# A decoder layer's FFN: the down projection in seven block products, with hidden values and weight forms in DRAM

## The chip, the cores and the metric

The kernel runs on one core of one Trainium2 chip, in one launch. The metric is the device time of that launch in microseconds (us); lower is better. The TensorE clock has two levels, 1.2 and 2.4 GHz; a granted clock of 1.00 in the profile is the upper one.

## What is computed

One inference step of a decoder layer on 1024 prompt tokens and 8 x 4 sample tokens, T = 1056 in all, width 1024, FFN width 2816, all in float32:

```python
m, sh, sr = _mixer(x, pos, ...)          # input projection, 4 HGRN2 heads, 4 retention heads, output projection
x = _layer_norm(ALPHA * x + m, ln1_g, ln1_b)
hidden = silu(x @ w_gate) * (x @ w_up)   # (T, 2816)
x = _layer_norm(ALPHA * x + hidden @ w_down, ln2_g, ln2_b)
```

The change lies in the FFN, that is in the last two lines.

## The kernel before

Activations stand transposed in SBUF, features over the 128 partitions and tokens along the row, in four quarters q of 264 tokens; two quarters make a half pr. A float32 product is made of three matmuls: each operand is split into a high part (a cast on ScalarE, L189) and a low part (a subtraction, L190, on GpSimd for weights and on VectorE for most else), and TensorE adds hi x hi, hi x lo and lo x hi into one PSUM tile. A matmul takes a 128 x 128 weight block and 264 columns.

The 2816 hidden features are 22 blocks of 128, worked off as 11 pairs p. For each pair the kernel computes gate and up values and then at once the pair's share of the down projection:

- Pair 0 computes gate and up plainly (`gu`).
- For pairs 1 to 10 `unit` (matmuls L910) computes gate, and again up, in the Strassen-Winograd form: the two feature blocks, the two halves of the 1024 inputs and the two quarters of a half make 2 x 2 blocks, and seven products A11 x B11, S2 x T2, S3 x T3, S1 x T1, A12 x B21, A22 x T4, S4 x B22 take the place of eight. Each product has 12 matmuls for each half, a unit 7 x 2 x 12 = 168. `blocks` loads two raw weight blocks into the three slots of `wr` and makes the block forms S1 to S4 on GpSimd (L885 to L892). The token forms T1 to T4 were made once; they lie in `X` and `XB`. The results are joined by `gate_fin` and `up_fin` on VectorE and ScalarE, and `up_fin` (L956 to L959) splits the hidden values h into 16 buffers.
- `down` (matmuls L988) loads the pair's w_down rows through `wdown`, which also subtracts each row's mean (L212 to L214), and multiplies: 8 output tiles x 4 quarters x 6 = 192 matmuls. VectorE adds every PSUM tile to the residual `Y` (L993 for the first pair, L995 after it).

Beside these rounds GpSimd centres the residual (`total` sums the eight tiles of a quarter, L774; after a matmul with the mean, `center` subtracts it, L780), one quarter in each of rounds 1 to 4. In the last pair the order is unit(half 0), `down` of quarters 0 and 1, unit(half 1), `down` of quarters 2 and 3; `squares` and `norm2` (matmuls L730 and L721, steps L819 to L826) compute the second normalization there and send it out.

The order on each engine is fixed when the program is built; a list `side` of generators, stepped by `tick` with a rate, mixes the side work in between the matmuls, and final steps go ahead of it by `tc.high_priority`. All DMAs are issued by SP's queue in its order. An engine works its instructions off in order, and each waits for its inputs and for its buffer.

```python
for p in range(1, NPAIR - 1):
    unit(blocks(a["w_gate"], 2 * p), (0, 1), gate_fin(h), RF)
    unit(blocks(a["w_up"], 2 * p), (0, 1), up_fin(h), RF)
    ...
    down(wdown(p), h, (0, 2, 1, 3), False, RF / 2)
```

Of the kernel before, what the change touches and what calls it, by code (L numbers as in the profile page):

```python
# [17 lines left out]
P = 128  # L18
# [11 lines left out]
NF = FF // P  # L30
CW = 352
# [16 lines left out]
HK = KT // 2  # L48
HP = 500
# [75 lines left out]
def body(tc, ctx, a):  # L125
# [26 lines left out]

    csts = [cst]
# [42 lines left out]
    def load_raw(src, shape=(P, KT, P)):  # L196
        raw = wp.tile(list(shape), F32, tag="wr", name="wr", bufs=3)
        nc.sync.dma_start(raw, src)
        return raw
# [6 lines left out]

    def load_w(src, shape=(P, KT, P), eng=None, cen=False, keep=None, dst=None):
        raw = load_raw(src, shape)
        if cen:
            flat = raw.rearrange("p k n -> p (k n)")  # L210
            mn = tmp.tile([P, 1], F32, tag="mn", name="mn", bufs=2)
            V.tensor_reduce(mn, flat, axis=AX, op=add)  # L212
            V.tensor_scalar(mn, mn, -1.0 / D, None, op0=mul)
            V.tensor_scalar(flat, flat, mn, None, op0=add)  # L214
        if keep is not None:
            keep.append(raw)
        h = shape[1] // 2
        return [block(raw[:, i * h:i * h + h], eng[i] if isinstance(eng, tuple) else eng, dst and dst[i]) for i in range(2)]
# [479 lines left out]
    with ExitStack() as ctxB:  # L698
# [72 lines left out]
        def total(q):  # L771
            zm[q] = ut()
# [11 lines left out]
        def squares(parts, engines, apart=0):  # L784
            def sq(m, y):
                n = len(seen)
                new = n < len(engines) or n >= KT - apart
                q2 = (tt("s2") if n == 0 else hid(F32)) if new else ut()
                S.activation(q2, y, AF.Square)
                if new:  # L790
                    parts.append(q2)
                else:
                    i = n % len(engines)
                    engines[i].tensor_tensor(parts[i], parts[i], q2, op=add)
                seen.append(m)

            seen = []
            return sq

        def norm2(q, parts, g, b, w1, w2, pool=(), last=False):  # L800
            sl = qs_(q)
            if pool:
                V.tensor_tensor(parts[0], parts[0], parts[1], op=add)
                parts.pop()
# [6 lines left out]
            if pool:  # L811
                rbs = ut()
                S.copy(rbs, rb)
            for m in range(KT):
                y = Y[:, m, sl]
                if m in PM and pool:
# [3 lines left out]
                if m in pool:  # L820
                    G.tensor_scalar(y, y, g[:, m:m + 1], b[:, m:m + 1], op0=mul, op1=add)
                elif last and m in TV:
# [6 lines left out]

        def both(*gens):  # L830
            gens = list(gens)
            while gens:
                for g in list(gens):
                    try:
                        next(g)
                        yield
                    except StopIteration:
                        gens.remove(g)
# [113 lines left out]
        def up_fin(h):  # L952
            def fin(i, j, pr, ps, u):
                g, f = h[i, 2 * pr + j], ut()
                if u is None:
                    V.tensor_tensor(f, ps, g, op=mul)  # L956
                else:
                    V.tensor_tensor(f, ps, u, op=add)
                    V.tensor_tensor(f, f, g, op=mul)  # L959
                h[i, 2 * pr + j] = hi, lo = hid(F32R), hid(F32R)  # L960
                split(hi, lo, f)
            return fin


        def gu(i, wg, wu, q, h, rate):
# [6 lines left out]
            h[i, q] = hi, lo = hid(F32R), hid(F32R)  # L972
            with tc.high_priority(offset=HP):
                S.activation(sg, po[0], AF.Silu)
                V.tensor_tensor(po[1], po[1], sg, op=mul)
                split(hi, lo, po[1])

        def down(wd, h, qs, first, rate, squares=None, banks=(pj, mx)):
            for j in (1, 0):
                for q in qs:  # L980
                    for mm in range(HK):
                        m = HK * j + mm
                        out = banks[mm % len(banks)]()[:, :CQ]
                        n = 0
                        for i in range(2):
                            hi, lo = wd[i][j]
                            for w, x in ((hi, 0), (hi, 1), (lo, 0)):
                                PE.matmul(out, w[:, mm], h[i, q][x], start=(n == 0), stop=(n == 5))  # L988
                                n += 1
                        y = Y[:, m, qs_(q)]  # L990
                        with tc.high_priority(offset=HP):
                            if first:
                                V.scalar_tensor_tensor(y, y, ALPHA, out, op0=mul, op1=add)  # L993
                            else:
                                V.tensor_tensor(y, y, out, op=add)  # L995
                            if squares is not None:
                                squares(m, y)
                        tick(rate)
# [28 lines left out]
        def wdown(p, **kw):  # L1027
            return [load_w(a["w_down"][2 * p + i].rearrange("p (k n) -> p k n", n=P), cen=True, **{k: v[i] for k, v in kw.items()}) for i in range(2)]

        NPAIR = NF // 2  # L1030
        h = {}
        ws = [[load_w(a[n][t]) for n in ("w_gate", "w_up")] for t in range(2)]
        for q in range(NQ):
# [3 lines left out]
            if q % 2:  # L1037
                side.insert(min(len(side), 1 if q == 1 else NQ), (("c1", q // 2), combine1(q // 2)))
        wd = wdown(0)
        for pr in range(2):  # L1040
            drain(("c1", pr))
            down(wd, h, (2 * pr, 2 * pr + 1), True, RB / 2, banks=(pj,))
        while step():
            pass
        for p in range(1, NPAIR - 1):
            h = {}
            if p <= NQ:
                side.append(("t", total(p - 1)))
            unit(blocks(a["w_gate"], 2 * p), (0, 1), gate_fin(h), RF)
            unit(blocks(a["w_up"], 2 * p), (0, 1), up_fin(h), RF)  # L1050
            while step():
                pass
            if p <= NQ:
                mu = mx()[:, :CQ]
                PE.matmul(mu, K_("mean"), zm[p - 1], start=True, stop=True)
                mc = ut()
                S.copy(mc, mu)
                side.append(("c", center(p - 1, mc)))
            down(wdown(p), h, (0, 2, 1, 3), False, RF / 2)

        p = NPAIR - 1
        h = {}
        unit(blocks(a["w_gate"], 2 * p), (0, 1), gate_fin(h), RF)
        w = blocks(a["w_up"], 2 * p)
        unit(w, (0,), up_fin(h), RF)
        wd = wdown(p, eng=((V, G), (V, G)), dst=[[[XB[:, hl, j, :, i * P:(i + 1) * P] for hl in range(2)] for j in range(2)] for i in range(2)])
# [6 lines left out]
        while step():  # L1073
            pass
# [73 lines left out]
```

## Time and profile before

| | |
|---|---|
| time, median of 3 runs | 1341.13 us (1340.98 to 1341.15) |
| profiled execution: own time, span | 1343.02 us, 1341.2 us |
| mean granted TensorE clock | 0.989 |
| busy: TensorE, VectorE, GpSimd, ScalarE | 1316.8, 769.7, 622.9, 470.0 us |
| DMA | 97.09 MB, 72 GB/s |
| last FFN matmul ends at | 1325.66 us of the span |

The busy times add up how long each engine had an instruction in work; they overlap. The chain is the work that ended last, followed backwards from the end, step by step to what released it; only what lies on it sets the time. Windows give the same busy times for a stretch of the span. A row of an instruction group names line, engine, operation, output and input, and how many there were. Engines: PE is TensorE (PEld its weight loads), DVE is VectorE, ACT ScalarE, POOL GpSimd, SP the queue that issues DMAs.

### The profile page before, as it was taken

Reading aid. Unit: us, or ns where it says so; the run is one execution under the profiler, and the core shown is the slowest. Engines: PE = TensorE matmul, PEld = TensorE weight load, DVE = VectorE, ACT = ScalarE, POOL = GpSimd, SP = SyncE. Lnnn points to the kernel's source line nnn. Section 1 sums busy time; section 2 is a strip of 40 time slices with the busy share of each in tenths; the row PEclk is TensorE's granted clock in tenths of the full one; section 3 lists DMA queues with packets and bytes.
Section 4 is the critical chain, followed back from the end, with each engine's and each line's share of the span. In section 5 each row is a group of like instructions: output and inputs, shape, how many; then the busy total and the mean of one; then the engine's idle time right before and its main releaser. Section 6 shows DMA issues by size and latency. Waiting matters only on the chain.

```text
span 1341.2 us, 28935 instructions
## 1 busy us (share of the span) xinstructions
PE 1316.8 (98%) x11886; PEld 1290.4 (96%) x11886; DVE 769.7 (57%) x1857; ACT 470.0 (35%) x1037; POOL 622.9 (46%) x572
## 2 busy tenths in 40 slices
PE   8999999999999999999999999999999999999995
PEld 7999999999999999999999999999999999999995
DVE  6255444666566673477656464656556464746466
ACT  6343442332322353366432323232313232322334
POOL 1862331321212155352586767766545545464443
PEclk8999999999999999999999999999999999999997
DMA  8344412203212117220120101111111111110112
GB/s 280 123 170 156 172 34 81 80 4 97 66 33 66 34 50 218 63 87 2 36 92 31 65 32 64 33 64 32 64 32 64 33 64 48 48 64 32 48 34 98
DMA packets 67508, 97.09 MB, mean 72 GB/s; under 512 B 5808, under 2 KB 52272, under 8 KB 67376
## 3 DMA queue, kind: packets, MB, share of 16 engines
q1 hardware_dynamic: 67376, 95.24, 21.9%
q8 instruction: 93, 1.52, 0.5%
q14 instruction: 39, 0.32, 0.1%
HBM read 77.66 MB, written 17.56 MB: 71 GB/s over the span
## 4 chain that ended last, share of the span: by engine, by line
PE 94%; DVE 2%; DMA 2%; ACT 1%; SPq 0%; issue 0%; POOL 0%; ACTq 0%; DVEq 0%
PE pj L232 36%; PE mx L910 17%; PE pj L910 14%; PE pj L988 12%; PE mx L988 8%; PE mx L458 1%; PE mx L601 1%; PE mx L571 1%; PE mx L603 1%; PE mx L553 1%; DMA M<-in_xT 1%; DMA Y<-xc 1%; PE mx L642 1%; PE mx L513 1%; DMA wr<-in_w_in 0%; PE mx L721 0%
## 5 line engine op out<-in xcount | busy, mean ns | idle before, releaser
L190 POOL TENSOR_TENSOR bl<-wr,bh 128x512 fp32r<-128x512 f32 x252 | 327.1, 1306 | 434.7 <-ACT bh L189 431.3
L232 PE MATMUL pj<-X,bh 128*128 128x352 f32 (+1 forms) x1936 | 428.9, 310 | 4.9 <-DVE q L378 3.4
L232 PEld LDWEIGHTS pj<-X,bh 128*128 128x128 f32 x1936 | 321.9, 189 | 9.6 <-issue 3.5
L232 PE MATMUL pj<-X,bl 128*128 128x352 f32 (+1 forms) x968 | 298.0, 308 | 0.1
L189 ACT CAST bh<-wr 128x512 fp32r<-128x512 f32 x260 | 158.1, 620 | 367.5 <-PE mx L988 166.8
L232 PEld LDWEIGHTS pj<-X,bl 128*128 128x128 f32 x968 | 183.0, 189 | 0.8 <-DVE bl L190 0.4
L988 PE MATMUL pj<-h,bh 128*128 128x264 f32 x704 | 135.5, 285 | 0.0
L910 PE MATMUL pj<-X,bh 128*128 128x264 f32 x672 | 125.6, 286 | 0.0
L910 PE MATMUL mx<-X,bh 128*128 128x264 f32 x608 | 112.9, 285 | 0.0
L910 PE MATMUL mx<-XB,bh 128*128 128x264 f32 x608 | 112.7, 284 | 0.0
L988 PE MATMUL mx<-h,bh 128*128 128x264 f32 x576 | 111.2, 285 | 0.0
L988 PEld LDWEIGHTS pj<-h,bh 128*128 128x128 f32 x704 | 109.3, 188 | 0.3
L910 PEld LDWEIGHTS pj<-X,bh 128*128 128x128 f32 x672 | 104.6, 189 | 0.1
L988 PE MATMUL pj<-h,bl 128*128 128x264 f32 x352 | 100.0, 284 | 0.0
L910 PE MATMUL pj<-X,bl 128*128 128x264 f32 x336 | 95.8, 285 | 0.0
L995 DVE TENSOR_TENSOR Y<-Y,pj 128x264 f32<-128x264 f32 x176 | 74.8, 426 | 36.3 <-PE pj L988 36.0
L910 PEld LDWEIGHTS mx<-XB,bh 128*128 128x128 f32 x608 | 94.1, 188 | 0.0
L910 PEld LDWEIGHTS mx<-X,bh 128*128 128x128 f32 x608 | 93.8, 188 | 0.0
L232 PE MATMUL pj<-bh,X 128*128 128x256 f32 x512 | 93.0, 280 | 0.0
L988 PEld LDWEIGHTS mx<-h,bh 128*128 128x128 f32 x576 | 89.3, 188 | 0.0
L910 PE MATMUL mx<-X,bl 128*128 128x264 f32 x304 | 86.0, 283 | 0.0
L910 PE MATMUL mx<-XB,bl 128*128 128x264 f32 x304 | 86.0, 284 | 0.0
(229 smaller groups left out, 2519.4 us busy)
## 6 DMA issues: line engine op xcount, KB each, us to landing
wr<-in_w_in SPq DMA_DIRECT2D x23, 512.0 KB, 3.8
wr<-in_w_gate SPq DMA_DIRECT2D x22, 512.0 KB, 3.2
wr<-in_w_up SPq DMA_DIRECT2D x22, 512.0 KB, 3.2
wr<-in_w_down SPq DMA_DIRECT2D x22, 512.0 KB, 3.3
wr<-wc SPq DMA_DIRECT2D x14, 512.0 KB, 4.1
M<-in_xT SPq DMA_DIRECT2D x24, 176.0 KB, 4.2
xc<-M SPq DMA_DIRECT2D x24, 176.0 KB, 2.0
Y<-xc SPq DMA_DIRECT2D x32, 132.0 KB, 3.4
```

The source lines that it names most:

```text
L189: S.copy(hi, src)
L190: (eng or V).tensor_tensor(lo, src, hi.bitcast(F32), op=sub)
L232: PE.matmul(out, l, r, start=(i == 0), stop=(i == n - 1))
L458: PE.matmul(into(B32 * b, (c % 4) * w), k[:, o:o + B32], cols(q, o), start=True, stop=True)
L513: PE.matmul(a_ps[:, c * C:(c + 1) * C], k[:, cc], q[:, cc], start=True, stop=True)
L553: PE.transpose(t_ps[:, c * C:(c + 1) * C], k[:, (4 * b + c) * C:(4 * b + c + 1) * C], ident)
L571: PE.matmul(d_ps[:, c * P:(c + 1) * P], tk[:, 4 * b + c], v[:, 4 * b + c], start=True, stop=True)
L601: PE.matmul(o[:, c * P:(c + 1) * P], at[:, cc], v[:, cc], start=True, stop=(cc == 0))
L603: PE.matmul(o[:, c * P:(c + 1) * P], q[:, cc * C:(cc + 1) * C], st[:, cc - 1], start=False, stop=True)
L910: PE.matmul(bank[pr], l[:, k], rs[k][r], start=(first and n == 0), stop=(n == 3 * HK - 1), skip_group_check=not first)
L988: PE.matmul(out, w[:, mm], h[i, q][x], start=(n == 0), stop=(n == 5))
L995: V.tensor_tensor(y, y, out, op=add)
```

## The change

- Gate and up of all pairs are computed first. `up_fin` leaves the hidden values whole, and after the last product of a half `kinds` makes seven block forms of them (B11, B21, B22, T1 to T4; four subtractions or additions on VectorE, tiles of 264 columns) and stores each in the DRAM buffer `hd`: 2 x 7 x 11 = 154 stores of 132 KB.
- `prep`, one step of it per `tick` of its generator, reads w_down twice: `rowsum` (the row means) and `forms`, which makes the seven block forms of the centred weights (four VectorE steps of 256 columns and three ScalarE biases for each half c of a pair) and stores them in the DRAM buffer `wb`: 154 stores of 128 KB in rows of 512 bytes.
- `down` and `wdown` are gone. After pair 10 the seven products run over all 11 pairs at once: for each product, half pr and output tile mm, 33 matmuls into one PSUM tile, which VectorE adds to one to four places in `Y`: 112 additions in place of 352. `wkind` loads the weight form in two pieces (8 and 3 pairs) and splits it on ScalarE and VectorE, into the two rings first and then into `X`. `hkind` loads the eleven tiles of a hidden form through the 16 `h` buffers and splits them on ScalarE and GpSimd into 24 slots of `XB`.
- `total` and `center` have a round each, p = 1 to 8, since `Y` doesn't change during the rounds. The last pair's special order is gone; the second normalization of quarters 0, 2 and 1 runs beside the last products (`ENDS`), that of quarter 3 after them. In pair 1 the gate unit runs half by half.

```diff
+DOWN = (
+    ("A11", "B11", ((0, 0), (0, 1), (1, 0), (1, 1))),
+    ("S2", "T2", ((1, 0), (0, 1), (1, 1))),
+    ("S3", "T3", ((1, 0), (1, 1))),
+    ("A12", "B21", ((0, 0),)),
+    ("A22", "T4", ((1, 0),)),
+    ("S1", "T1", ((1, 1), (0, 1))),
+    ("S4", "B22", ((0, 1),)),
+)
+ENDS = {(4, 0): 0, (4, 1): 2, (6, 0): 1}
...
+    hd = dram.tile([7, 2, NPAIR, P, CQ], F32, name="hd")
+    wb = dram.tile([7, HK, P, NPAIR, P], F32, name="wb")
...
-        def up_fin(h):
+        def up_fin(h, p):
...
-                h[i, 2 * pr + j] = hi, lo = hid(F32R), hid(F32R)
-                split(hi, lo, f)
+                    V.tensor_tensor(g, f, g, op=mul)
+                if (i, j) == (0, 1):
+                    kinds(p, pr, h)
             return fin
+        def kinds(p, pr, h):
+            b11, b21, b12, b22 = [h[i, 2 * pr + j] for j in range(2) for i in range(2)]
+            def put(n, src):
+                nc.sync.dma_start(hd[KH.index(n), pr, p], src)
+            put("B11", b11)
+            put("B21", b21)
+            put("B22", b22)
+            t3, t2, t4 = [hid(F32) for _ in range(3)]
+            V.tensor_tensor(t3, b22, b12, op=sub)
+            put("T3", t3)
+            V.tensor_tensor(t2, t3, b11, op=add)
+            put("T2", t2)
+            V.tensor_tensor(b12, b12, b11, op=sub)
+            put("T1", b12)
+            V.tensor_tensor(t4, b21, t2, op=sub)
+            put("T4", t4)
...
+        def forms(p, c):
+            m1, m2, m12 = mns[p]
+            raw = wp.tile([P, 2, 2, 2, P], F32, tag="wr", name="wr", bufs=3)
+            for i in range(2):
+                nc.sync.dma_start(raw[:, i], a["w_down"][2 * p + i].rearrange("p (j c m n) -> p j c m n", j=2, c=2, n=P)[:, :, c])
+            a11, a21, a12, a22 = [raw[:, i, j] for i in range(2) for j in range(2)]
...
+            V.scalar_tensor_tensor(s1, a21, m12, a22, op0=add, op1=add)
+            put("S1", s1)
+            V.tensor_tensor(a21, a11, a21, op=sub)
+            put("S3", a21)
+            yield
+            for x, mn, n in ((a22, m2, "A22"), (a12, m2, "A12"), (a11, m1, "A11")):
+                S.activation(x, x, AF.Identity, bias=mn)
+                put(n, x)
+            V.tensor_tensor(s2, a22, a21, op=sub)
+            put("S2", s2)
+            yield
+            V.tensor_tensor(s4, a12, s2, op=sub)
+            put("S4", s4)
...
+        def hkind(n, pr):
+            out = []
+            for r in range(NPAIR):
+                raw = hid(F32)
+                nc.sync.dma_start(raw, hd[n, pr, r])
...
+                split(hi, lo, raw, G)
...
+        for p in range(1, NPAIR):
+            h = {}
+            q, back = divmod(p - 1, 2)
+            if q < NQ:
+                side.append(("c", center(q, mc) if back else total(q)))
+            side.append(("w", forward()))
+            w = blocks(a["w_gate"], 2 * p)
+            for prs in ((0,), (1,)) if p == 1 else ((0, 1),):
+                unit(w, prs, gate_fin(h), RF)
+            side.append(("w", forward()))
+            unit(blocks(a["w_up"], 2 * p), (0, 1), up_fin(h, p), RF)
...
+        for n, (wn, hn, to) in enumerate(DOWN):
+            ws = [wkind(KW.index(wn), mm) for mm in range(HK)]
+            for pr in range(2):
+                hs = hkind(KH.index(hn), pr)
+                for mm in range(HK):
+                    out = pj()[:, :CQ]
+                    i = 0
+                    for (wh, wl), (xh, xl) in zip(ws[mm], hs):
+                        for l, r in ((wh, xh), (wh, xl), (wl, xh)):
+                            PE.matmul(out, l, r, start=(i == 0), stop=(i == 3 * NPAIR - 1))
...
+                        for jm, jt in to:
+                            m, q = HK * jm + mm, 2 * pr + jt
+                            y = Y[:, m, qs_(q)]
...
+                                V.tensor_tensor(y, y, out, op=add)
```

Three places show the new order. In the rows below a line number is that of the changed kernel; L215 is `load_raw`, L961 a store of `kinds`, L1071 a load of `hkind`, and x22 means 22 such instructions in a row.

SP at the end of the FFN, before the change (the last pair's loads and all that follows):

```order
L198 DMA wr<-in_w_down 128x1024 x2
L198 DMA wr<-in_w_gate 128x1024 x2
L198 DMA wr<-in_w_up 128x1024 x2
L198 DMA wr<-in_w_down 128x1024 x2
L826 DMA out_yT<-Y 128x264 x32
```

SP after the change, from the last weight forms' loads to the first loads of hidden forms:

```order
L215 DMA wr<-wb 128x384
L961 DMA hd<-h 128x264 x2
L215 DMA wr<-wb 128x1024
L215 DMA wr<-wb 128x384
L961 DMA hd<-h 128x264 x2
L215 DMA wr<-wb 128x1024
L961 DMA hd<-h 128x264 x3
L1071 DMA h<-hd 128x264 x22
L215 DMA wr<-wb 128x384
L215 DMA wr<-wb 128x1024
L215 DMA wr<-wb 128x384
L1071 DMA h<-hd 128x264 x19
```

Before, nothing follows the last weight loads but the output. Now the 22 loads of the first product's hidden tiles stand behind the last stores of `kinds`, and loads of `wb` stand between those stores.

VectorE after the change, around the end of the last up unit; L950 and L951 are `up_fin`, L967, L969, L971 and L973 the four steps of `kinds`, L207 a low part. The last unit matmul is what the L950 here waits for:

```order
L967 TENSOR_TENSOR h<-h 128x264
L207 TENSOR_TENSOR X<-wr,X 128x1024
L950 TENSOR_TENSOR u<-mx,u 128x264
L969 TENSOR_TENSOR h<-h 128x264
L971 TENSOR_TENSOR h<-h 128x264
L207 TENSOR_TENSOR X<-wr,X 128x384
L951 TENSOR_TENSOR h<-u,h 128x264
L207 TENSOR_TENSOR X<-wr,X 128x1024
L973 TENSOR_TENSOR h<-h 128x264
L967 TENSOR_TENSOR h<-h 128x264
L207 TENSOR_TENSOR X<-wr,X 128x384
L969 TENSOR_TENSOR h<-h 128x264
```

L971 and L973 follow, and four more low parts, ahead of the first addition to `Y` (L1165). Before, L959 and the split of the hidden values stood in this place. `kinds` of both halves and the low parts of the first weight forms now share VectorE there.

GpSimd in a middle round after the change; L876 to L878 and L883 are the four weight combinations of `blocks` (f1, a21, a11 of the next weights, and S4), L784 is `total`, L790 `center`:

```order
L207 TENSOR_TENSOR bl<-wr,bh 128x512 x2
L784 TENSOR_TENSOR s_11733<-Y 128x264
L790 TENSOR_TENSOR Y<-Y,s_11103 128x264 x8
L883 TENSOR_TENSOR wr<-wr 128x512
L784 TENSOR_TENSOR s_11733<-s_11733,Y 128x264
L207 TENSOR_TENSOR bl<-wr,bh 128x512
L784 TENSOR_TENSOR s_11733<-s_11733,Y 128x264
L207 TENSOR_TENSOR bl<-wr,bh 128x512
L784 TENSOR_TENSOR s_11733<-s_11733,Y 128x264
L876 TENSOR_TENSOR s_11391<-wr 128x512
```

The same place before the change (L885 to L892 are the combinations, L780 is `center`):

```order
L190 TENSOR_TENSOR bl<-wr,bh 128x512 x2
L887 TENSOR_TENSOR wr<-s_11739,wr 128x512
L190 TENSOR_TENSOR bl<-wr,bh 128x512 x2
L190 TENSOR_TENSOR bl<-s_11739,bh 128x512
L780 TENSOR_TENSOR Y<-Y,u 128x264 x7
L190 TENSOR_TENSOR bl<-wr,bh 128x512
L780 TENSOR_TENSOR Y<-Y,u 128x264
L190 TENSOR_TENSOR bl<-wr,bh 128x512
L892 TENSOR_TENSOR wr<-wr 128x512
L885 TENSOR_TENSOR s_11984<-wr 128x512
L886 TENSOR_TENSOR wr<-wr 128x512
```

In both, `center` stands ahead of the S4 combination. Now its eight steps are in one row with the first step of the next quarter's `total` ahead of it, and the other steps of `total` are mixed in between the low parts and the next weights' combinations behind it.

## Rows read from the trace of the kernel before

**Rows 1.** The page: busy time by engine, and the chain's shares.

```profile
PE 1316.8 (98%) x11886; PEld 1290.4 (96%) x11886; DVE 769.7 (57%) x1857; ACT 470.0 (35%) x1037; POOL 622.9 (46%) x572
...
PE 94%; DVE 2%; DMA 2%; ACT 1%; SPq 0%; issue 0%; POOL 0%; ACTq 0%; DVEq 0%
```

**Rows 2.** Windows: stretch, length, busy us of PE, PEld, DVE, ACT, POOL, clock, DMA share, GB/s.

```profile
0.00:23.60 23.60, 17.92 (x90) 14.15 (x91) 15.40 (x32) 16.31 (x34) 2.62 (x8) 0.98 0.94 308
...
863.00:927.60 64.60, 64.60 (x532) 64.53 (x531) 35.99 (x74) 18.46 (x40) 44.91 (x41) 1.00 0.15 50
...
1248.90:1341.20 92.30, 76.43 (x583) 74.83 (x581) 55.80 (x161) 39.35 (x88) 38.11 (x42) 0.88 0.18 59
```

**Rows 3.** The chain, in order of time: start, us, what.

```profile
1012.33 5.84 PE pj L910 x48
...
1324.08 1.58 PE pj L988 x12
```

**Rows 4.** Timeline of PE at the last handover: start, us; in brackets the wait before.

```profile
1304.97 0.83 PE L721 MATMUL mx<-cst,rs 128*128 128x128 f32 x6 [2.27 <-DVE rs L225]
...
1309.54 1.36 PE L988 MATMUL pj<-h,XB 128*128 128x264 f32 x4 [1.34 <-ACT h L189]
```

**Rows 5.** Windows of PE after these waits: length, busy us, clock, DMA share, GB/s.

```profile
1306.00:1311.00 5.00, 3.56 (x16) 0.52 0.23 81
1311.00:1313.00 2.00, 1.88 (x8) 0.50 0.44 138
...
1315.00:1317.00 2.00, 2.00 (x13) 0.64 0.42 141
```

**Rows 6.** Instruction groups, 733 to 1260 us: busy us, mean ns, idle before.

```profile
L190 POOL TENSOR_TENSOR bl<-wr,bh 128x512 fp32r<-128x512 f32 x132 | 172.0, 1309 | 170.0 <-ACT bh L189 169.9
...
L189 ACT CAST bh<-wr 128x512 fp32r<-128x512 f32 x132 | 80.2, 620 | 238.2 <-PE mx L988 158.8 <-PE pj L910 38.0 <-PE mx L910 31.2
...
L995 DVE TENSOR_TENSOR Y<-Y,mx 128x264 f32<-128x264 f32 x129 | 55.1, 427 | 29.2 <-PE mx L988 28.8 <-POOL s L885 0.3
...
L189 ACT CAST h<-u 128x264 fp32r<-128x264 f32 x64 | 25.9, 413 | 72.7 <-DVE u L959 57.0 <-DVE u L956 15.4
...
L780 POOL TENSOR_TENSOR Y<-Y,u 128x264 f32<-128x264 f32 x24 | 18.0, 778 | 0.5 <-DVE Y L995 0.5
L774 POOL TENSOR_TENSOR u<-u,Y 128x264 f32<-128x264 f32 x18 | 15.1, 840 | 0.2
```

**Rows 7.** VectorE's groups by shape, whole span: low parts of 352 and 512 columns.

```profile
L959 DVE TENSOR_TENSOR u<-u,h 128x264 f32<-128x264 f32 x60 | 45.1, 752 | 0.7
...
L190 DVE TENSOR_TENSOR X<-M,X 128x352 fp32r<-128x352 f32 x24 | 11.4, 523 | 1.4 <-ACT X L189 1.4
...
L190 DVE TENSOR_TENSOR bl<-wr,bh 128x512 fp32r<-128x512 f32 x8 | 5.3, 690 | 6.2 <-ACT bh L189 6.2
```

**Rows 8.** The instructions of L959: shortest, median and longest in ns.

```profile
L959 DVE TENSOR_TENSOR u<-u,h x60: 418/429/1583, 699.9 to 1310.3; 128x264 f32<-128x264 f32 x60
```

**Rows 9.** DMA issues: count, KB each, median us from issue to landing.

```profile
wr<-in_w_up SPq DMA_DIRECT2D x22, 512.0 KB, 3.2
...
wr<-wc SPq DMA_DIRECT2D x14, 512.0 KB, 4.1
...
Y<-xc SPq DMA_DIRECT2D x32, 132.0 KB, 3.4
out_yT<-Y SPq DMA_DIRECT2D x32, 132.0 KB, 1.8
...
wc<-wr SPq DMA_DIRECT2D x8, 512.0 KB, 3.3
```

**Rows 10.** Timeline of POOL in a middle round: start, us, wait before and its releaser.

```profile
908.24 5.24 POOL L780 TENSOR_TENSOR Y<-Y,u 128x264 f32<-128x264 f32 x7
916.23 1.29 POOL L190 TENSOR_TENSOR bl<-wr,bh 128x512 fp32r<-128x512 f32 x1 [2.74 <-ACT bh L189]
...
922.65 1.29 POOL L885 TENSOR_TENSOR s<-wr 128x512 f32<-128x512 f32 x1 [1.92 <-DMA wr<-in_w_up]
```

More of the change, by code (lines that the diff above doesn't have):

```diff
@@ L30 @@
 NF = FF // P
+NPAIR = NF // 2
 CW = 352
@@ L217, in load_w @@
         h = shape[1] // 2
-        return [block(raw[:, i * h:i * h + h], eng[i] if isinstance(eng, tuple) else eng, dst and dst[i]) for i in range(2)]
+        return [block(raw[:, i * h:i * h + h], eng) for i in range(2)]
     def newton(dst, var, y, t):
@@ L810, in norm2 @@
             rb = spread(rs, CQ)
-            if pool:
+            if not last:
                 rbs = ut()
@@ L815, in norm2 @@
                 y = Y[:, m, sl]
-                if m in PM and pool:
+                if m in PM and not last:
                     G.tensor_tensor(y, y, rbs, op=mul)
@@ L971, in gu @@
             sg = ut()
-            h[i, q] = hi, lo = hid(F32R), hid(F32R)
+            f = h[i, q] = hid(F32)
             with tc.high_priority(offset=HP):
                 S.activation(sg, po[0], AF.Silu)
[L975 to L998, printed above, removed]
@@ L1037, in body, with forward @@
             if q % 2:
+                kinds(0, q // 2, h)
                 side.insert(min(len(side), 1 if q == 1 else NQ), (("c1", q // 2), combine1(q // 2)))
[L1039 to L1042, printed above, removed]
+        work = prep()
+        def forward():
+            for x in work:
+                yield
+                if x:
+                    return
+        for p in range(1, NPAIR):
[9 more added lines that the diff above has]
+            unit(blocks(a["w_up"], 2 * p), (0, 1), up_fin(h, p), RF)
+            while step():
+                pass
+            if q < NQ and not back:
+                mu = mx()[:, :CQ]
+                PE.matmul(mu, K_("mean"), zm[q], start=True, stop=True)
+                mc = tt("s2")
+                S.copy(mc, mu)
@@ L1043, in body @@
         while step():
             pass
[L1045 to L1066, printed above, removed]
-        sums = [[] for _ in range(NQ)]
-        for q in range(2):
-            down(wd, h, [q], False, 1.0, squares(sums[q], (V, G)), banks=(pj,))
-            side.append(("n2", norm2(q, sums[q], l2g, l2b, 1, 4, PM)))
@@ L1071, in body @@
-        unit(w, (1,), up_fin(h), RE)
-        down(wd, h, [2], False, RF, squares(sums[2], (V, G)), banks=(pj,))
-        while step():
-            pass
-        n2, n3 = norm2(2, sums[2], l2g, l2b, 1, 9, (7,)), norm2(3, sums[3], l2g, l2b, 0, 1, last=True)
-        side.append(("n2", n2))
-        down(wd, h, [3], False, 1.0, squares(sums[3], (V,), 1), banks=(pj,))
-        next(n3)
-        for x in list(n2) + list(n3):
+        for x in norm2(NQ - 1, l2g, l2b, last, 0, 0, True):
             pass
```

144 lines of the change are left out of this document (98 added, 46 removed).

## The prediction

> **What bounds the kernel now.** I read the busy times first: TensorE 98%, no other engine above 57%, and the chain that ended last is 94% TensorE [rows 1]. So the time is the number of matmuls times what one takes, plus the few places where TensorE stands still. The windows of single pairs say the same: in a round of 64.6 us TensorE is busy throughout at granted clock 1.00 (the 2.4 GHz level), GpSimd 45 us (one of those that centre a quarter), VectorE 36, ScalarE 18, the DMA engines 15% [rows 2]. The chain gives the price of one matmul of 264 columns: 48 in 5.84 us, 121.7 ns [rows 3]. A pair is 336 block matmuls and 192 of `down`, 528 x 0.1217 = 64.26 us. The only large gap of the FFN is near the end, where the last unit hands over to `down`: waits of 2.27 and 1.34 us [rows 4], and clock 0.52 and 0.50 (the 1.2 GHz level) after them until it rises between 1315 and 1317 us [rows 5]. From 1248.9 us to the last matmul's end at 1325.66 (1324.08 + 1.58 in [rows 3]) lie 76.76 us against 64.26 of matmuls: 12.5 too many. About 4 of these are the normalization's small matmuls and the work between; 8.5 I put down to the stall and the low clock.
>
> **The change part by part.** Durations are those of the profiled execution, whose own time is 1343.02 us: a span of 1341.2 and 1.8 around it, which the change leaves. The runs without a profile have a median of 1341.13; I subtract from that, and a profiled execution of the changed kernel should read 1.9 more.
>
> *Matmuls.* `down` had 11 pairs x 192 = 2112; the seven products have 7 x 2 halves x 4 tiles x 33 = 1848. That is 264 fewer at 121.7 ns, and TensorE is the bound: **-32.1 us**. The old handover inside the last pair goes with `down`: **-8.5**.
>
> *Evictions.* 352 additions into `Y` become 112, 240 x 0.427 us [rows 6] less on VectorE, off the path. It is spent again: per pair 8 subtractions for the hidden values (`kinds`), 8 for the weight forms, two row sums. Nothing of it counts while VectorE has room in a round.
>
> *The new handover.* After the last unit come `down`'s first inputs, the eleven blocks of the sum's first product, out of DRAM. SP's order puts every read of `hd` behind the last store of `hd`, so the first waits for the last subtraction on VectorE. Let t be the end of the last unit matmul. VectorE then has one eviction and product (0.43 each), seven SBUF subtractions (0.43 alone, as the L959 row's median, up to the mean 0.75 beside GpSimd) and weight subtractions of 1024, 384 and 384 columns [rows 6 to 8]. From 352 columns in 0.52 and 512 in 0.69 the slope is 1.04 ns per column: 1.22 and 0.56. Together 0.86 + 3.0 + 2.34 = 6.2 alone and 8.4 beside GpSimd; I take 8.4, since GpSimd is working there. The read lands 3.4 later (the row of a 132 KB load [rows 9]), the cast is 0.41, GpSimd's subtraction 0.76 [rows 6]: first tile at t+13.0. Ten more tiles at 0.76 put the eleventh at t+20.6, three matmuls end it at t+21.0; unhindered this sum of 33 would end at t+4.0. **+17**, between 11 (6.2 on VectorE, half of the tiles subtracted while the first is awaited) and 24 (the first cast waits in ScalarE's queue behind two weight loads, 2 x 3.2). TensorE idles for long there, and in the trace a wait of 2.27 and 1.34 us was followed by some 9 us at half clock [rows 4, 5]; here part of such a stretch falls on matmuls that wait for tiles anyway: **+2**, between 0 and 5.
>
> *The rounds.* A round is now 336 x 0.1217 = 40.9 us instead of 64.3, but GpSimd keeps its 22 weight operations (28.8 us at 1.309), and `center` and `total` add 8 x 0.778 + 7 x 0.840 = 12.1 per two rounds: 34.8 of 40.9. It fits. The lead is what matters. `wr` has three slots, and w_down's raw forms now pass through them between the gate and up loads. Let t be the end of an up unit. VectorE finishes the products and `kinds` at about t+4.7 (eleven steps of 0.43), four weight steps at t+6.4; the stores land 1.8 later, at t+8.2, and then the next up weights load in 3.2: t+11.4 [rows 9]. GpSimd's five operations up to S2's low part are 6.6, ScalarE's two casts 1.2 [rows 6], with some 1.1 for handovers: t+20.3. It is wanted for the second product of the next up unit, t + 8 x 2.92 = t+23.4: 3 us to spare, where before the change GpSimd could wait for a cast or a load on the way, 1.9 and 2.7 us at a time, with nothing lost on TensorE [rows 10]. In three rounds GpSimd's order puts eight centring steps into this path; seven took 5.24 us in a block [rows 10], so eight take 6.0, and 2.9 are missing: **+9**, between 0 and 30 (1.5 us in every unit).
>
> *DMA.* A round moves 7.9 MB (2.1 of gate and up, 2.1 of w_down read twice, 1.9 of stores to `hd`, 1.8 to `wb`): 193 GB/s, where the trace shows 308 in the first stretch at a share of 0.94 [rows 2]. Covered, at nothing; the price if it isn't is in the second rival. In the last phase a product of full length takes 264 x 0.1217 = 32.1 us and reads 5.9 MB (182 GB/s); GpSimd has 22 x 0.76 = 16.7 us of it, ScalarE 22 casts of 0.41 and four pairs of 1.05 and 0.51 (0.83 ns per column from the two casts of [rows 6]), 15.3: also covered. The first pair's missing `down` costs 0 to 2 us, since its up weights are asked for sooner. The last normalization (15.5 us from the last matmul to the end of the span) stays as it is: 0.
>
> Sum: -32.1 - 8.5 + 17 + 2 + 9 = **-12.6**, so **1328.5 us**.
>
> **The rivals.** *First, the rounds lose nothing and the handover is short* (11, no half clock): -32.1 - 8.5 + 11 = 1311.5 us. For it: 3 us of lead, and the median of L959 is the uncontended 0.43. Against it: the reads' place in SP's order.
>
> *Second, slower: the raw-weight loop is late in every unit.* Place: `wr`'s slot between a form's store and the next load. Price: without the +9 the sum stands at -21.6 over 20 units, so it decides from 1.1 us per unit on. Take VectorE's subtractions at the contended 0.75 (8 x 0.32 = 2.6), the stores at the 3.3 of the largest store in the trace instead of 1.8 (+1.5), the loads at the 4.1 of those out of DRAM buffers instead of 3.2 (+0.9) [rows 9]: 5.0 against 3 us of lead, 2.0 missing, 20 x 2.0 = +40, 1359.5 us. For it: three slots only, with 38 DMAs of a round in SP's one queue where there were six. Against: the three delays don't fall together every time.
>
> *Third, VectorE and GpSimd exclude each other.* What the trace shows: L959, with two inputs in SBUF, takes 418 to 1583 ns with median 429 [rows 8], and GpSimd's steps stay at 1.29 to 1.31 [rows 6, 10]: so far VectorE pays, and GpSimd hardly does. If the two serialize, a round has 34.8 us of GpSimd plus 22 such VectorE steps (8 `kinds`, 8 forms, 6 products) x 0.43 = 9.5: 44.3 against 40.9, 3.4 late in each of eight rounds, +27 in place of +9: 1346.5 us. Before, 45 + 14 x 0.43 = 51 of 64.6 left room, so no row of it could have shown a loss. The Trainium skill has this as a rule ("SBUF — State Buffer", section "Who interferes with whom"): the two share a port pair, an exclusive lock, and a VectorE instruction with two SBUF inputs blocks or is blocked by a GpSimd one that reads SBUF, by order of issue. By that rule the sum would be this rival's; the trace agrees in the 1583 ns, and shows no GpSimd step lengthened as much.
>
> **How the numbers follow.** Forecast 0.42; first rival 0.20; second 0.15; third 0.10; the remaining 0.13 is a handover at its upper bounds (24 + 5) with the rounds at 5 to 9, 1334.5 to 1338.5 and a little more. A measurement of this kernel tells 0.2%, 2.7 us, from no change. Faster: 0.42 + 0.20 + 0.10 of the remainder = 0.72; slower: 0.15 + 0.06 of the third + 0.01 of the remainder = 0.22; the rest of the third (a part of the steps avoid each other) and of the remainder, 0.04 + 0.02 = 0.06, is the same. The range goes from below the first rival (a handover of 9, 1309) to above the third (1350), leaving out the most of the second; the forecast's own range is 1319 (rounds at 0) to 1336 (handover at 24).
>
> **What would show it.** Right: 1848 matmuls at the new product's line, 122 ns each in the chain; gate and up rounds of 41 to 43 us, GpSimd busy 34 to 36 in them; one gap of 15 to 20 us in TensorE before the first product, released by GpSimd, with SP's first `hd` read issued after the last `hd` store. Wrong: rounds of 45 us or more, with GpSimd waiting for a `wr` load (second rival) or back to back without waiting (third); matmuls above 125 ns in the last phase; or a gap there that ends by a weight cast on ScalarE.

## The result, and the profile after

The changed kernel takes **1420.49 us** (median of 4 runs, 1416.91 to 1422.19), the kernel before 1341.14: a ratio of 1.0585, 95% interval 1.0572 to 1.0599. It is 79 us slower, where 13 us faster was forecast, and outside the range. The profiled execution has a span of 1414.8 us.

The page, busy time by engine as in [rows 1]:

```profile
PE 1307.9 (92%) x11622; PEld 1276.2 (90%) x11622; DVE 793.9 (56%) x1759; ACT 527.7 (37%) x1192; POOL 688.5 (49%) x666
```

The 264 matmuls are gone (11622 in place of 11886), but TensorE's share has fallen from 98% to 92%, and its busy time by 9 us only. Where it went is read from the windows of the FFN's stages, columns as in [rows 2]: pair 1; the stretch after it; pairs 2 to 10; the handover with the first four sums of 33; the other products; the tail.

```profile
645.40:689.50 44.10, 43.04 (x350) 42.41 (x348) 26.62 (x57) 16.21 (x40) 21.70 (x17) 1.00 0.56 167
689.50:710.70 21.20, 0.01 (x1) 0.01 (x1) 13.91 (x21) 2.41 (x5) 11.81 (x14) 0.52 0.68 216
710.70:1139.80 429.10, 393.06 (x3030) 386.75 (x3030) 248.58 (x425) 131.96 (x296) 295.21 (x237) 0.96 0.52 163
1139.80:1187.80 48.00, 18.18 (x132) 17.89 (x133) 30.23 (x32) 22.04 (x48) 25.04 (x35) 0.73 0.79 233
1187.80:1401.10 213.30, 213.28 (x1748) 213.30 (x1749) 99.45 (x218) 91.09 (x208) 105.04 (x127) 0.99 0.50 150
1401.10:1414.80 13.70, 3.30 (x24) 3.12 (x22) 7.07 (x26) 7.88 (x16) 2.84 (x4) 0.60 0.46 158
```

Three of the six lose. After pair 1 TensorE stands still for 21.2 us. The nine pairs 2 to 10 take 429.1 us, where 9 x 40.9 = 368 would do: 61 lost, of which TensorE waits 36 (429.1 - 393.1) and works 25 too long. The handover takes 48.0 us for 132 matmuls worth 16.1: 32 lost. The products themselves run as forecast: 1716 matmuls and the normalization's in 213.3 us, TensorE busy throughout.

The waits of TensorE on the whole span, by releaser (total us, how many, longest):

```profile
PE pj L901 <- ACT bh L206: 47.5, 11, 21.2
PE pj L1156 <- ACT XB L206: 21.0, 1, 21.0
PE pj L1156 <- DVE Y L1165: 8.8, 1, 8.8
```

The 21.2 us are those after pair 1. SP's rows there:

```profile
699.91 3.88 SPq L961 DMA_DIRECT2D hd<-h  x5
...
704.86 0.92 SPq L215 DMA_DIRECT2D wr<-in_w_gate  x2
```

The gate weights of pair 2 are asked for behind the last hidden stores of pair 1. L901 is the units' matmul, L206 the cast and L207 the low part of `split`, L1156 the products' matmul. So the units wait for casts of weights. One of these waits, the 5.00 us at 933.74, followed back. The last matmul of the up unit, which ends at 902.7 us, and on VectorE what is worked off around and behind it (start, us, instruction, wait before; L951 is the product of `up_fin`, L967 to L973 are `kinds`, L994 the row sum):

```profile
902.45 0.28 PE L901 MATMUL mx<-X,bl 128*128 128x264 f32 x1
```
```profile
902.35 1.40 DVE L967 TENSOR_TENSOR h<-h 128x264 f32<-128x264 f32 x1
903.68 0.42 DVE L950 TENSOR_TENSOR u<-mx,u 128x264 f32<-128x264 f32 x1
904.02 1.17 DVE L969 TENSOR_TENSOR h<-h 128x264 f32<-128x264 f32 x1
905.12 1.52 DVE L971 TENSOR_TENSOR h<-h 128x264 f32<-128x264 f32 x1
906.56 1.52 DVE L951 TENSOR_TENSOR h<-u,h 128x264 f32<-128x264 f32 x1
908.01 1.53 DVE L973 TENSOR_TENSOR h<-h 128x264 f32<-128x264 f32 x1
...
912.17 0.98 DVE L973 TENSOR_TENSOR h<-h 128x264 f32<-128x264 f32 x1
913.08 0.76 DVE L912 TENSOR_TENSOR u<-pj,u 128x264 f32<-128x264 f32 x2
917.19 1.22 DVE L994 TENSOR_REDUCE mn<-wr 128x1 f32<-128x1024 f32 x1 [3.36 <-DMA wr<-in_w_down]
...
920.78 0.43 DVE L1031 TENSOR_TENSOR u<-wr,u 128x256 f32<-128x256 f32 x1
```

A step of this size takes 0.42 us where one input is in PSUM (L950) and 0.98 to 1.53 in the lines here where both are in SBUF. GpSimd hardly pauses in this stretch. `kinds` ends at 913.1, 10.4 us after the unit's last matmul and not 4.7; in the pairs 2 to 9 it ends 5.6 to 11.3 us after it. SP waits with it (start, us):

```profile
900.97 12.53 SPq L961 DMA_DIRECT2D hd<-h  x11
913.59 0.38 SPq L215 DMA_DIRECT2D wr<-in_w_down  x1
918.44 0.33 SPq L215 DMA_DIRECT2D wr<-in_w_up  x1
...
923.63 0.34 SPq L215 DMA_DIRECT2D wr<-in_w_up  x1
```

The load for the row sum stands behind the eleven stores and goes out at 913.59, 0.4 us after the last subtraction; the two up loads follow as slots come free. The first of them goes out at 918.44, when the reduction of the row sum has just ended, and VectorE's four weight steps stand behind that reduction too: the last of them (L1031) ends at 921.2, 18.5 us after the unit. So the row sum is a second link of this chain, with 3.36 us of waiting and 1.22 of work. Each of the pairs 2 to 7 shows it: VectorE waits 3.0 to 3.8 us for the load, and an up load goes out as the reduction ends. GpSimd can begin its combinations only at 927.55, does `total` in between, and TensorE has run dry:

```profile
927.55 1.29 POOL L876 TENSOR_TENSOR s<-wr 128x512 f32<-128x512 f32 x1 [2.08 <-DMA wr<-in_w_up]
928.79 0.74 POOL L784 TENSOR_TENSOR s<-s,Y 128x264 f32<-128x264 f32 x1
...
931.60 1.44 POOL L878 TENSOR_TENSOR wr<-s,wr 128x512 f32<-128x512 f32 x1
```
```profile
933.74 1.25 PE L901 MATMUL pj<-XB,bh 128*128 128x264 f32 x4 [5.00 <-ACT bh L206]
```

A part of the other 25 us is the clock. After the two longer waits of this stretch (5.00 and, at 979.86, 2.27 us) the granted clock is 0.66 in a slice of 10 us: 29 matmuls in 6.3 us of busy time and 51 in 9.2, where a full slice has 84:

```profile
930.00:940.00 10.00, 6.26 (x29) 6.26 (x30) 4.15 (x5) 5.03 (x13) 9.97 (x9) 0.66 0.28 79
...
960.00:970.00 10.00, 10.00 (x84) 10.00 (x83) 6.97 (x9) 0.62 (x1) 5.15 (x4) 1.00 0.48 161
...
980.00:990.00 10.00, 9.16 (x51) 8.95 (x52) 2.82 (x6) 4.49 (x11) 9.00 (x7) 0.66 0.57 175
```

So a wait costs its length and, at the lower level after it, a part of that again. How much, the mean clock of 0.96 over the 429.1 us bounds: 4% of them, by its rounding 15 to 19 us, and less as far as TensorE stood still at the lower level. At least 6 of the 25 us are something else: matmuls that follow each other more slowly at the upper level, which no view here divides further.

At the handover the same two engines meet in a sharper form. VectorE, GpSimd and TensorE there:

```profile
1171.80 14.51 DVE L207 TENSOR_TENSOR X<-wr,X 128x384 fp32r<-128x384 f32 x1 [10.59 <-ACT X L206]
```
```profile
1160.85 25.04 POOL L207 TENSOR_TENSOR XB<-h,XB 128x264 fp32r<-128x264 f32 x35 [30.25 <-ACT XB L206]
```
```profile
1160.83 0.81 PE L1156 MATMUL pj<-XB,bh 128*128 128x264 f32 x2 [21.04 <-ACT XB L206]
...
1187.82 0.78 PE L1156 MATMUL pj<-XB,bh 128*128 128x264 f32 x2 [8.80 <-DVE Y L1165]
```

A subtraction of 384 columns, 0.55 us elsewhere, begins at 1171.80 and ends at 1186.31, 0.4 us after the last of 35 subtractions that GpSimd does without a gap. Behind it the first additions to `Y` wait, the four sums that are done stay in PSUM, and TensorE waits 8.80 us more. In the 30.25 us in which GpSimd waits before that run, VectorE's steps with both inputs in SBUF take 0.43 us, the four of `kinds` as well as L951, which took 1.52 us above. At L951 TensorE is busy and the DMA share 0.80:

```profile
1135.22 0.43 DVE L951 TENSOR_TENSOR h<-u,h 128x264 f32<-128x264 f32 x1
```
```profile
1130.00:1140.00 10.00, 9.79 (x79) 9.44 (x77) 5.63 (x12) 3.55 (x6) 0.60 (x1) 1.00 0.80 232
```

So it is GpSimd that lengthens these steps, and not TensorE or the DMAs beside them.

### The profile page after: what moved, and what is told of

Read it like the earlier page. It is cut to its first block, busy times and chain, and to the rows that moved or that the text cites. A ratio compares the mean times of both kernels' runs of the same rounds, so it can differ in the third digit from the quotient of the medians.

```text
span 1414.8 us, 29994 instructions
## 1 busy us (share of the span) xinstructions
PE 1307.9 (92%) x11622; PEld 1276.2 (90%) x11622; DVE 793.9 (56%) x1759; ACT 527.7 (37%) x1192; POOL 688.5 (49%) x666
## 2 busy tenths in 40 slices
DMA packets 173789, 190.71 MB, mean 135 GB/s; under 512 B 14800, under 2 KB 154960, under 8 KB 173648
## 5 line engine op out<-in xcount | busy, mean ns | idle before, releaser
L207 POOL TENSOR_TENSOR bl<-wr,bh 128x512 fp32r<-128x512 f32 x212 | 279.9, 1333 | 366.2 <-ACT bh L206 347.8
L206 ACT CAST bh<-wr 128x512 fp32r<-128x512 f32 x226 | 134.6, 617 | 236.9 <-PE pj L242 67.6
L1156 PE MATMUL pj<-XB,X 128*128 128x264 f32 x1716 | 210.6, 285 | 0.0
L1156 PEld LDWEIGHTS pj<-XB,X 128*128 128x128 f32 x1716 | 209.2, 189 | 0.0
L207 POOL TENSOR_TENSOR XB<-h,XB 128x264 fp32r<-128x264 f32 x154 | 123.3, 842 | 108.2 <-ACT XB L206 108.2
L901 PE MATMUL pj<-X,bh 128*128 128x264 f32 x672 | 126.3, 288 | 21.2 <-ACT bh L206 21.2
L901 PEld LDWEIGHTS pj<-X,bh 128*128 128x128 f32 x672 | 105.0, 190 | 21.8 <-ACT bh L206 21.6
L901 PE MATMUL mx<-XB,bh 128*128 128x264 f32 x608 | 114.6, 288 | 2.5 <-DVE mn L995 1.9
L901 PE MATMUL mx<-X,bh 128*128 128x264 f32 x608 | 114.3, 288 | 0.2 <-DVE mn L995 0.2
L901 PE MATMUL pj<-XB,bh 128*128 128x264 f32 x352 | 76.2, 317 | 26.3 <-ACT bh L206 26.3
L901 PEld LDWEIGHTS mx<-XB,bh 128*128 128x128 f32 x608 | 95.5, 192 | 3.4 <-DVE mn L995 2.5
L1026 ACT ACTIVATE wr<-wr,mn 128x256 f32<-128x256 f32 x66 | 32.5, 508 | 174.8 <-DMA wr<-in_w_down 83.0
L242 PE MATMUL pj<-bh,X 128*128 128x256 f32 x512 | 96.5, 284 | 0.0
L901 PE MATMUL pj<-X,bl 128*128 128x264 f32 x336 | 95.3, 286 | 0.1
L901 PEld LDWEIGHTS mx<-X,bh 128*128 128x128 f32 x608 | 94.5, 190 | 0.6 <-DVE mn L995 0.5
L207 DVE TENSOR_TENSOR X<-wr,X 128x1024 fp32r<-128x1024 f32 (+1 forms) x52 | 65.6, 1270 | 46.2 <-ACT X L206 35.8
L901 PEld LDWEIGHTS pj<-XB,bh 128*128 128x128 f32 x352 | 63.0, 218 | 28.5 <-ACT bh L206 28.5
L901 PE MATMUL mx<-X,bl 128*128 128x264 f32 x304 | 85.9, 285 | 1.8 <-POOL bl L207 1.8
```

Of the source, the lines that this page charges most:

```text
L206: S.copy(hi, src)
L207: (eng or V).tensor_tensor(lo, src, hi.bitcast(F32), op=sub)
L242: PE.matmul(out, l, r, start=(i == 0), stop=(i == n - 1))
L901: PE.matmul(bank[pr], l[:, k], rs[k][r], start=(first and n == 0), stop=(n == 3 * HK - 1), skip_group_check=not first)
L1026: S.activation(x, x, AF.Identity, bias=mn)
L1156: PE.matmul(out, l, r, start=(i == 0), stop=(i == 3 * NPAIR - 1))
```

## The experiments

Theory A: the path of the weights is late because VectorE's steps with two SBUF inputs wait for GpSimd, and SP's queue passes this on to the loads. Rivals: B, the volume of the DMAs and the three slots of `wr`; C, GpSimd's centring in the path. Differences are against the changed kernel's 1420.5 us. The expectations name some runs by number; e6, e11 and e12 are marked below.

**The first weight forms earlier.** Two steps of `prep` run beside pair 0:

```diff
-                    if 2 * p + c > 1:
-                        yield True
+                    yield True
...
                 side.insert(min(len(side), 1 if q == 1 else NQ), (("c1", q // 2), combine1(q // 2)))
...
+                side.append(("w", forward()))
```

> The first two weight-form halves are made beside pair 0, so that the first round after it makes one half per unit like every other round, and the gate weights of pair 2 are asked for sooner. Theory A (SP's queue: loads stand behind stores that wait for VectorE): the 21.2 us wait after pair 1 shrinks to a few us, the clock stays up, -20 to -27 us against the changed kernel, some 1395 us. Rival (the raw-weight loop is limited by slots and DMA volume, so the loss only moves): -5 us or less.

Measured: 1409.73 us, -11. The wait of 21.2 us is replaced by four of 6.2, 2.6, 1.6 and 1.1 us, where A expected a few us in all. This falls between the two expectations: the backlog of forms was a part of that wait only.

**`kinds` without its subtractions.**

```diff
-            V.tensor_tensor(t3, b22, b12, op=sub)
-            put("T3", t3)
...
+            put("T3", b22)
...
```

> Leaves out the four VectorE steps of kinds per half (plain blocks are stored in place of T1 to T4), with the same 14 stores per round. Theory A (kinds runs at half speed beside GpSimd and holds the stores, and behind them SP's loads): rounds 4 us shorter or more, and the wait after pair 1 shorter too, -35 to -55 us. Rival B (volume of the DMAs, number of wr slots): 0 to -8 us, since neither changes.

Measured: 1352.32 us, -68: more than either expected. The waits of the rounds shrink, but so does the handover's, from 21.0 to 3.3 us; since three `h` buffers per half came free too, this run alone doesn't say which of the two counted.

**No centring.**

```diff
-            if q < NQ:
-                side.append(("c", center(q, mc) if back else total(q)))
...
```

> Leaves out total and center (12 us of GpSimd per two rounds). Rival C (GpSimd's centring in the path of the weights): all waits of the rounds go, -45 us or more. Theory A: GpSimd frees VectorE a little and its part of the path, 2 to 3 us per round, -15 to -25 us, and the wait after pair 1 stays at 15 us or more.

Measured: 1391.28 us, -29: more than the 25 that A allows and far from C's 45. Another expectation of A failed: the wait after pair 1 fell to 5.9 us, probably because the block of eight centring steps, beside which `kinds` ran there, was gone.

**No row sums.**

```diff
-            raw = load_raw(a["w_down"][2 * p + i].rearrange("p (k n) -> p k n", n=P))
...
-            V.tensor_reduce(mn, raw.rearrange("p k n -> p (k n)"), axis=AX, op=add)
-            V.tensor_scalar(mn, mn, -1.0 / D, None, op0=mul)
+            V.memset(mn, 0.0)
```

> Leaves out the row sums: no second read of w_down, 22 loads of 512 KB, 22 uses of a wr slot and 22 reductions fewer; the means are taken as zero. Rival B (slots and volume): the rounds lose hardly anything, -45 us or more. Theory A: the loads of gate and up still stand behind the hidden stores, -10 to -30 us.

Measured: 1364.91 us, -56, which is what B expected and A did not (-10 to -30). But the row sum is also a link of the chain above (SP's load at 913.59, VectorE's wait of 3.36 and 1.22 us), so volume and chain had to be told apart by runs that change one of them.

**`kinds` as copies on ScalarE** (e6). Steps, buffers and stores stay:

```diff
-            V.tensor_tensor(t3, b22, b12, op=sub)
+            S.copy(t3, b22)
...
```

> The four steps of kinds become copies on ScalarE, one after the other as before and into the same buffers; the stored T blocks are plain copies, not the sums. So the number of steps, buffers and stores stays, and only VectorE's two-input reads beside GpSimd go. Theory A1 (the steps take twice their time beside GpSimd, and VectorE's queue is late behind them): most of what leaving them out gave, -35 to -60 us. Rival A2 (what counted in leaving them out were the three buffers per half that came free, so that reads could run ahead at the handover): 0 to -15 us, and the wait before the first down product stays near 21 us.

Measured: 1354.47 us, -66. Nearly all of what leaving the steps out gave, with the same volume and the same buffers. So it is the steps of `kinds` on VectorE; whether their number or their length beside GpSimd counts, the run with one input in PSUM tells. The wait before the first product, which A2 put near 21 us, fell to 7.7. The wait after pair 1 is still 14.8 us.

**Hidden tiles loaded straight into `XB`.**

```diff
-                raw = hid(F32)
-                nc.sync.dma_start(raw, hd[n, pr, r])
...
+                raw = lo.bitcast(F32)
+                nc.sync.dma_start(raw, hd[n, pr, r])
```

> Hidden tiles are loaded straight into the place of their low part in XB and split there, so their loads need no h buffer; nothing else is changed. Theory A2: the handover (21.0 us of waiting, 8.8 behind VectorE's 14.5 us subtraction, and the low clock after them) nearly goes, -25 to -33 us, and the rounds stay. Theory A1 alone: the reads still stand behind the last stores, -5 us or less.

Measured: 1386.33 us, -34. SP's order now has the first tiles' loads ahead of the last stores, and the first product shows waits of 0.6, 1.2 and 0.8 us. The rounds are as before. So the handover can be mended without the rounds, by the buffers that A2 names. They are not its only cause: the copies on ScalarE shortened it too, with the buffers as they were.

**`kinds` with one input in PSUM.** The same idea with all four sums kept; the products stay in their banks, and the next gate unit takes the banks in another order:

```diff
+                    V.tensor_tensor(ps, ps, g, op=mul)
+                    pp[i, 2 * pr + j] = ps
+                    if j == 0:
+                        S.copy(g, ps)
...
-            V.tensor_tensor(t3, b22, b12, op=sub)
+            x11, x21, x12 = [pp.get(k, h[k]) for k in ((0, 2 * pr), (1, 2 * pr), (0, 2 * pr + 1))]
+            V.tensor_tensor(t3, b22, x12, op=sub)
```

> Correct form of e6's idea: the products of three of the four blocks stay in PSUM, ScalarE copies two of them for their stores, and each step of kinds then has one input in PSUM. Theory A1: these steps take 0.43 to 0.5 us beside GpSimd, kinds ends 5 us sooner, -20 to -40 us. Rival A2: -5 to +5 us, since buffers and order stay.

Measured: 1368.43 us, -52, more than expected. VectorE's groups from 720 to 1130 us (busy us, mean ns, idle before), the third and first step of `kinds` in the changed kernel, then the same two here:

```profile
L971 DVE TENSOR_TENSOR h<-h 128x264 f32<-128x264 f32 x16 | 18.3, 1144 | 0.0
...
L967 DVE TENSOR_TENSOR h<-h 128x264 f32<-128x264 f32 x16 | 16.6, 1040 | 0.3
```
```profile
L981 DVE TENSOR_TENSOR h<-mx,h 128x264 f32<-128x264 f32 x18 | 7.7, 425 | 0.0
...
L977 DVE TENSOR_TENSOR h<-h,mx 128x264 f32<-128x264 f32 x18 | 7.6, 424 | 0.3
```

The same subtraction of the same size, 1040 and 1144 ns with both inputs in SBUF, 424 with one in PSUM. GpSimd's low parts meanwhile took 1362 ns in the changed kernel and 1332 here, against 1309 in [rows 6], its centring steps 878 and 788 against 778: VectorE pays most of it.

What these runs give back in each stage, in us of the profiled executions: the ten pairs from the first unit matmul to the last, and the handover from there to the start of the fifth sum.

| | ten pairs | handover |
|---|---|---|
| at 121.7 ns per matmul | 409 | 16 |
| changed kernel | 493 | 48 |
| first forms earlier | 480 | 47 |
| `kinds` without its subtractions | 456 | 22 |
| `kinds` as copies on ScalarE | 456 | 26 |
| `kinds` with one input in PSUM | 460 | 33 |
| no centring | 466 | 47 |
| no row sums | 451 | 37 |
| hidden tiles straight into `XB` | 492 | 21 |

In the pairs `kinds` is worth 33 to 37 us of the 84 lost, and most of it by the length of VectorE's steps, since the run in PSUM keeps them there (it leaves more products of `up_fin` with one input in PSUM, too). The row sums are worth 42 there, and centring 27.

**Low parts of the hidden tiles on VectorE.**

```diff
-                split(hi, lo, raw, G)
+                split(hi, lo, raw)
```

> In the seven products the low parts of the hidden tiles are subtracted on VectorE instead of GpSimd; nothing else is changed. If VectorE's 14.5 us subtraction came from GpSimd's 35 subtractions in a row, no subtraction of 384 columns takes over 1 us any more, the 8.8 us wait after the first products and the low clock behind it go, and eleven tiles at 0.43 instead of 0.72 us come sooner: -10 to -15 us. If the 14.5 us were a load's or ScalarE's lateness: 0 to -3 us.

Measured: 1405.75 us, -15. The 8.80 us wait is gone, and VectorE's subtractions into `X` (shortest, median, longest ns) are, in the changed kernel and here:

```profile
L207 DVE TENSOR_TENSOR X<-wr,X x52: 545/1219/14511, 1140.3 to 1362.7; 128x1024 fp32r<-128x1024 f32 x26, 128x384 fp32r<-128x384 f32 x26
```
```profile
L207 DVE TENSOR_TENSOR X<-wr,X x52: 548/886/1227, 1140.4 to 1352.0; 128x1024 fp32r<-128x1024 f32 x26, 128x384 fp32r<-128x384 f32 x26
```

**Three mends together** (e11): early forms, PSUM steps, direct loads.

> The early weight forms, the PSUM steps and the direct loads together. If their gains add up: -11 - 30 - 29 = -70 us, 1350 us; if they share one cause, no more than the largest of them.

Measured: 1344.16 us over 10 runs, ratio to before 1.002 (1.0001 to 1.0039), -76. The single gains sum to 97; they share the waits. The two longest that are left, 6.0 and 3.9 us, lie in rounds with centring.

**Centring beside the products** (e12). `total` stays, `center` moves behind the first product, with its mean times ALPHA; the `h` buffers go from 16 to 14:

```diff
-                side.append(("c", center(q, mc) if back else total(q)))
+                if not back:
+                    side.append(("c", total(q)))
...
+                if n == 0:
+                    for q in (2 * pr, 2 * pr + 1):
+                        side.append(("c", center(q, mcs[q])))
```

> The three changes of e11, and center is moved out of the rounds into the seven products (its mean scaled like Y by then). Theory A1 (what is left in e11 is GpSimd's time against VectorE's and the path of the weights; the two longest waits, 3.9 and 6.0 us, stand in rounds with centring): -10 to -18 us against e11, 1326 to 1334 us, faster than both kernels. Rival (rest is SP's queue): 0 to -4.

Measured: 1331.25 us, ratio to before 0.9932 (0.9917 to 0.9947), 13 less than the run above.

**w_down loaded once.** `forms` takes both halves from two whole blocks:

```diff
-        def forms(p, c):
...
-            raw = wp.tile([P, 2, 2, 2, P], F32, tag="wr", name="wr", bufs=3)
+        def forms(p):
+            raws, ms = [], []
             for i in range(2):
...
+                raw = load_raw(a["w_down"][2 * p + i].rearrange("p (k n) -> p k n", n=P))
```

> As e12, but each pair of w_down blocks is loaded once whole, in two loads that stay in two of the three wr slots until sums and forms are done, in place of the second read. Theory of the volume and the slots' number (rival B): another -10 us. Theory A1 with SP's queue: the second gate load stands behind 14 stores of forms in SP's order, so no better than e12 or worse, 1325 to 1350.

Measured: 1410.66 us, 79 more than the run above and outside both expectations, with less volume (179.18 in place of 190.73 MB); that goes against B's volume. SP's rows and the wait that follows, here:

```profile
853.87 0.44 SPq L1020 DMA_DIRECT2D wb<-u  x1
854.36 0.49 SPq L215 DMA_DIRECT2D wr<-in_w_gate  x1
```
```profile
863.73 1.25 PE L904 MATMUL pj<-XB,bh 128*128 128x264 f32 x4 [9.85 <-ACT bh L206]
```

The second gate load stands behind the last store of the forms, and every round waits 3 to 10 us. Since the two blocks hold two of the three slots until that store, this run doesn't tell SP's order from the number of slots.

**Hidden low parts on VectorE, all but the first product's**, on top of the late centring:

```diff
-                split(hi, lo, raw, G)
...
+                split(hi, lo, raw, V if n else G)
```

> As e12, with the low parts of the hidden tiles of all products but the first on VectorE. VectorE's own steps and GpSimd's centring then meet less: between -4 and +4 us against e12, as the last phase shows hardly any waits on TensorE already.

Measured: **1327.13 us**, ratio to before 0.9898 (0.9886 to 0.9911): the fastest version, 13 us less than the kernel before, 93 less than the changed one and 4 less than with the late centring alone. Its rounds in one window:

```profile
690.00:1080.00 390.00, 380.70 (x3072) 377.78 (x3071) 222.27 (x456) 152.06 (x352) 279.58 (x222) 0.99 0.61 194
```

It moves the volume of the changed kernel (190.73 against 190.71 MB) in shorter rounds, at a DMA share of 0.61 and 194 GB/s where the changed kernel's rounds had 0.52 and 163. So the DMA engines had room, and rival B's volume is out. The number of slots was not tried by itself and stays open, as up loads did go out when a slot came free.

## Why the prediction was wrong

The profiled execution took 1416.91 us where the forecast amounts to 1330.4 (1343.02 - 12.6). Of the 86.5 us between them 21 lie in the first pair's term, 52 in the rounds and 13 in the handover.

- *Matmuls, -32.1.* Right: 1140 of the products take 140.13 us in the chain, 122.9 ns each.
- *The old handover, -8.5.* Right as far as the trace shows: its place is gone.
- *The first pair's missing `down`, 0 to 2 us.* Wrong: 21.2. I looked at the up weights only. `prep` makes three halves of forms in the first unit and one in each later one, and the gate weights of pair 2 stand behind all of these and behind 14 hidden stores in SP's order. They went out at 704.86, 15 us after TensorE had run dry. The backlog is not all of it: without centring 5.9 us of the wait are left, with `kinds` as copies 14.8.
- *The rounds, +9.* This step failed by most: 61 for nine rounds. The chain was the one described, with three slots and 3 us to spare, but two of its links were wrong. The first was too short: "VectorE finishes the products and `kinds` at about t+4.7 (eleven steps of 0.43)". It was t+10.4, since the steps took 0.9 to 1.5 us; that alone uses up the 3 us nearly twice. The second was missing: the row sum, whose load stands behind the stores of `kinds` and whose reduction stands ahead of the weight steps and holds a slot that an up load waits for. Together with the wait it is 4.6 us, and the prediction has the row sums only among the steps of which it says "Nothing of it counts while VectorE has room in a round". So the four weight steps ended at t+18.5, not at t+6.4. I had the contended price of 0.75 in hand, a mean over places where GpSimd was often idle; I used it for the handover, where GpSimd turned out idle, and in a rival, but not in the rounds.
- *The two slower rivals were one.* The second gave 40 us for the late loop, with the subtractions at 0.75; the third had the exclusion, but let GpSimd carry it, at 0.43 per step in GpSimd's time. As far as `kinds` goes, what happened is the third's cause in the second's place: VectorE pays, and SP's queue turns it into late loads. The Trainium skill's rule ("SBUF — State Buffer", section "Who interferes with whom"), that two SBUF inputs on VectorE and a GpSimd instruction that reads SBUF exclude each other, agrees with 424 against 1040 ns.
- *The clock* was counted at the handover and left out of the rounds, where it took 15 to 19 us at most after waits of a few us each.
- *The handover, +17 and +2.* Measured 32 in the first 48 us. The last step of `kinds` ended at t+13.9, not t+8.4: its steps were at 0.43 here, with GpSimd idle, but VectorE came to the last product only at t+8.1, since the weight low parts ahead of it in its queue waited for loads of `wb`. The read landed 5.4 us after its issue, not 3.4. And the 14.5 us subtraction was in no bound.
- *DMA, covered.* Right, by the last run. *The tail, 0.* 13.7 in place of 15.5 us.

What stays open: how the loss of the pairs divides between `kinds`, row sum and centring. Alone they give back 37, 42 and 27 of 84 us; together that is more than was lost, so they share waits, probably since each puts the same few us of lead back. What a fourth slot of `wr` would give stays open too.

## What to carry to other kernels

Where a round is shortened, the engines beside the bound keep their work and lose their slack: price each of their steps by what it takes while its neighbour is busy, not by the mean of a longer round. A VectorE step with two SBUF inputs beside a busy GpSimd should have one input left in PSUM, and loads shouldn't stand in a queue behind stores that wait for such a step. A lead of a few us is little: one link priced too short and one left out used it up, and the waits that followed were paid in part a second time in the clock.

## What was not expected of the hardware

VectorE did not take turns with GpSimd: one subtraction of 0.55 us lasted 14.51 us, as long as the rest of a run of 35 GpSimd instructions without a gap, while in the rounds, where GpSimd's steps take 1.3 us, VectorE's took 0.9 to 1.5 us, as if each waited for one of them. GpSimd's own steps rose far less, its low parts from 1309 to 1362 ns and its centring steps from 778 to 878. That the exclusion is one of reads is only what the runs suggest: the step with one input in PSUM, which writes SBUF as the other does, was not delayed.
